# An unused table of 192 bytes ahead of the weight buffers: where the weights lie in SBUF

## The chip, the cores and the metric

The kernel runs on one core of a Trainium2 chip, in float32, one launch. The metric is the device time of the launch in microseconds (us). The numbers below come from the kernel's times and from one profiled execution of it.

## What is computed

Two transformer blocks over 256 tokens of width 1024. The first has chunked attention over 16 heads beside a gated linear recurrence, then a SwiGLU feed-forward; the second has four SwiGLU feed-forwards, a gated spatial mixing and a stick-breaking attention. Cut to its matrix products:

```python
u  = rmsnorm(x, g) @ w_in                       # 1024 x 7168
ya = chunked_band_attention(q, k, v) @ w_attn_out
yb = (rg_lru(conv(xr)) * gelu(gr)) @ w_rnn_out
h  = x + (g_a * ya + g_b * yb) @ w_o
gu = rmsnorm(h, g2) @ w_ffn_in                  # 1024 x 5632
h  = h + (silu(gu[:, :2816]) * gu[:, 2816:]) @ w_ffn_out
# second block: four more such feed-forwards, chunked_sgu (1024 x 4096, 2048 x 1024),
# k, v = rms_norm(x) @ w_kv, stick_breaking_attention(q, k, v) @ b_w_o, last rms_norm
```

## The kernel before

All weights pass through the core once. `PLAN` cuts them into 240 groups of 1 MB, each two chunks of 128 x 1024 floats. `load` (line 142) brings one group into one of three `raw` buffers by a DMA on SP's queue. `prep` (line 152) splits a chunk: ScalarE writes `h`, the rounded part (line 165), VectorE writes `l`, the rest (line 166), both as float32r. There are eight `h` and eight `l` buffers of 4096 bytes a partition; `prep` runs up to seven chunks ahead of the matmuls.

Activations are split the same way: into `xh` and `xl` (the normed input of a stage) and into the four `rr` tables (the input of an output projection). Each product of a chunk is three matmuls on line 213 (`mm3`, and the loops of `pe_nat` and `pe_rn`): h times h, h times l, l times h. They stand in two ways:

- `pe_k`, `pe_a` and `pe_r` **load the weights**, 128 x 128 of `h` or `l`, into the array and stream 256 columns of activations.
- `pe_nat` and `pe_rn` **stream the weights**, 512 columns of `h` or `l`, past 128 x 128 loaded activations. The feed-forwards' input projections (with the last one's output projection), the value projection and the spatial mixing's first half go this way. The stage of `kv_emit` loads weights in half of its matmuls and streams 256 columns of them in the other half.

The order is written by hand: each engine gets its instructions in the order of the code, and generators (`spawn`, `rounds`) put the work on finished stages between the chunks. TensorE reads a chunk once its `h` and `l` are ready, and ScalarE writes a buffer anew once the matmuls on its old content are done.

Every tile of the pool `const` gets its bytes of a partition in the order in which the code asks for it, rounded up to 32 bytes; the pools `raw` and `hl` follow behind it. So the sizes of the small tables ahead decide where the large buffers start. Before, these are the starting bytes in each partition, and what is left over a multiple of 512:

| tile | starts at | over a multiple of 512 |
|---|---|---|
| `x0` to `x3`, `xh`, `xl`, `rr0` to `rr3`, `sa` | 17408 to 74752 | 0 |
| `sb` to `sh`, `ident`, `ones` | 83072 to 132736 | 128 |
| `ntri`, `nones` (asked for after `setup`) | 136672, 137184 | 480 |
| three `raw` buffers of 8192 bytes | from 138816 | 64 |
| eight `h`, eight `l` buffers of 4096 bytes | from 163392, 196160 | 64 |

Every slice of these that a matmul reads starts a multiple of 512 bytes behind its tile's start.

Of the kernel before, what the change touches and what calls it, by code (L numbers as in the profile page):

```python
# [109 lines left out]
class Builder:  # L110
# [210 lines left out]
    def setup(self):  # L321
        nc, dram = self.nc, self.dram
        self.P = self.sb("par", [128, 224])[:, 0:NPAR]
        self.X = [self.sb(f"x{p}", [128, 2, 256]) for p in range(4)]
        self.XS = (self.sb("xh", [128, 8, 256], F32R), self.sb("xl", [128, 8, 256], F32R))
        self.RR = [self.sb(f"rr{i}", [128, 8, 256], F32R) for i in range(4)]
        self.SA = self.sb("sa", [128, 2080])[:, 0:8 * 259]
        self.SL = {c: self.sb("s" + c, [128, 2048]) for c in "bcdfgh"}
        self.ident = self.sb("ident", [128, 128])
        self.ones = self.sb("ones", [128, 128])  # L330
        self.mhalf = self.sb("mhalf", [128, 2])
        self.Rt = self.sb("rt", [128, 256])
        self.R1 = self.sb("r1t", [128, 256])
        self.Rkv = self.sb("rkv", [128, 256])
        self.rckv = self.sb("rckv", [128, 2])
        self.v2 = self.sb("v2", [128, 2])
        self.rc = self.sb("rc", [128, 2])
        self.tiny = self.sb("tiny", [128, 1])
        self.rc05 = self.sb("rc05", [128, 2])
        self.c8 = self.sb("c8", [128, 8])  # L340
        self.nc8 = self.sb("nc8", [128, 8])
        self.half = self.sb("half", [128, 24])
        self.sq = self.view("b", 4)
        nc.scalar.dma_start(self.P, dram["par"])
        x_load = lambda p: nc.sync.dma_start(self.X[p], dram["x"][:, 2 * p:2 * p + 2, :])
        for f in range(2):
            nc.sync.dma_start(self.X[0][:, f, :], dram["x"][:, f, :])
        self.warm_up()
        for g in range(2):
            t = self.rawp.tile([128, 2048], F32, tag="raw", name="raw")  # L350
            for c in range(2):
                if 2 * g + c:
                    x_load(2 * g + c)
                n = 512 if 2 * g + c == 0 else 1024
                for o in range(c * 1024, (c + 1) * 1024, n):
                    nc.sync.dma_start(t[:, o:o + n], dram["w"][g, :, o:o + n])
            self.raw[g] = t
        self.loads = 2
        self.load()
        self.gw = self.SL["h"].rearrange("p (a b) -> p a b", b=128)  # L360
        make_identity(nc, self.ident)
        nc.gpsimd.memset(self.ones, 1.0)
        nc.gpsimd.memset(self.mhalf, -0.5)
        nc.gpsimd.memset(self.tiny, 2.0 ** -115)
# [1041 lines left out]
```

## Time and profile before

| | us |
|---|---|
| median of 3 runs | 1444.81 |
| lowest, highest of the 3 | 1444.66, 1446.23 |
| the profiled execution | 1445.04 |
| its span, first to last instruction | 1443.3 |
| TensorE busy in the span | 1431.0 |

The mean granted clock of TensorE over the span was 0.998 of its 2.4 GHz. The page and the views name an operation as line, engine, operation, result <- inputs. For a matmul the streamed operand stands before the loaded one: `wk<-xh,h` streams `xh` past loaded `h`, `wk<-h,xh` streams `h` past loaded `xh`. The duration of one matmul is longer than the distance to the next start, since matmuls are pipelined; the pace is read from starts, or from a piece of the chain of work: its length over its count.

### The profile page before, as it was taken

Reading aid. Unit: us, or ns where it says so; the run is one execution under the profiler, and the core shown is the slowest. Engines: PE = TensorE matmul, PEld = TensorE weight load, DVE = VectorE, ACT = ScalarE, POOL = GpSimd, SP = SyncE. Lnnn points to the kernel's source line nnn. Section 1 sums busy time; section 2 is a strip of 40 time slices with the busy share of each in tenths; the row PEclk is TensorE's granted clock in tenths of the full one; section 3 lists DMA queues with packets and bytes.
Section 4 is the critical chain, followed back from the end, with each engine's and each line's share of the span. In section 5 each row is a group of like instructions: output and inputs, shape, how many; then the busy total and the mean of one; then the engine's idle time right before and its main releaser. Section 6 shows DMA issues by size and latency. Waiting matters only on the chain.

```text
span 1443.3 us, 21730 instructions
## 1 busy us (share of the span) xinstructions
PE 1431.0 (99%) x9112; PEld 1277.2 (88%) x9112; DVE 875.1 (61%) x1102; ACT 732.0 (51%) x985; POOL 21.4 (1%) x57
## 2 busy tenths in 40 slices
PE   8999999999999999999999999999999999999998
PEld 8998989888888888898999888898888898888886
DVE  6976688655547555566775554457555477644453
ACT  5777465544445544455444544446444467544442
POOL 0000000000000000000000000000000000000000
PEclk9999999999999999999999999999999999999999
DMA  7555545554553545546444555545554542445440
GB/s 296 197 193 200 186 160 195 188 201 175 184 195 147 204 176 180 209 151 224 171 168 155 222 185 180 191 154 204 186 193 176 183 168 88 161 176 193 186 175 30
DMA packets 37602, 259.98 MB, mean 180 GB/s; under 512 B 4224, under 2 KB 4608, under 8 KB 7040
## 3 DMA queue, kind: packets, MB, share of 16 engines
q1 hardware_dynamic: 36288, 253.77, 48.3%
q0 software_dynamic: 1072, 4.72, 1.0%
q8 instruction: 71, 1.16, 0.3%
q14 instruction: 27, 0.22, 0.0%
q10 hardware_dynamic: 144, 0.10, 0.0%
HBM read 257.53 MB, written 1.05 MB: 179 GB/s over the span
## 4 chain that ended last, share of the span: by engine, by line
PE 97%; DVE 1%; DMA 0%; ACT 0%; issue 0%; POOL 0%; SPq 0%; POOLq 0%; DVEq 0%; ACTq 0%
PE wk L213 60%; PE acc L213 35%; PE wk L755 2%; DMA raw<-w 0%; DVE l L166 0%; PE acc L525 0%; ACT h L165 0%; DVE sd L275 0%; DVE sb L275 0%; PE wk L525 0%; POOL r1c L283 0%; ACT sf L1020 0%; DVE sf L1011 0%; ACT sd L1010 0%; DVE sa L747 0%
## 5 line engine op out<-in xcount | busy, mean ns | idle before, releaser
L166 DVE TENSOR_TENSOR l<-raw,h 128x1024 fp32r<-128x1024 f32 (+1 forms) x479 | 572.7, 1220 | 317.2 <-ACT h L165 316.7
L165 ACT ACTIVATE h<-raw 128x1024 fp32r<-128x1024 f32 (+1 forms) x479 | 495.3, 1053 | 303.5 <-PE wk L213 192.7
L213 PE MATMUL wk<-h,xh 128*128 128x512 f32 x912 | 361.9, 397 | 0.0
L213 PE MATMUL wk<-h,xl 128*128 128x512 f32 x912 | 359.6, 394 | 0.0
L213 PE MATMUL wk<-l,xh 128*128 128x512 f32 x912 | 359.2, 394 | 0.0
L213 PE MATMUL acc<-rr,h 128*128 128x256 f32 x2016 | 358.5, 281 | 0.0
L213 PEld LDWEIGHTS acc<-rr,h 128*128 128x128 f32 x2016 | 307.9, 188 | 3.6 <-issue 1.9
L213 PE MATMUL acc<-rr,l 128*128 128x256 f32 x1008 | 281.2, 279 | 0.0
L213 PEld LDWEIGHTS wk<-h,xl 128*128 128x128 f32 x912 | 171.8, 188 | 39.4
L213 PEld LDWEIGHTS wk<-l,xh 128*128 128x128 f32 x912 | 171.9, 189 | 37.2
L213 PEld LDWEIGHTS wk<-h,xh 128*128 128x128 f32 x912 | 171.9, 188 | 36.8
L213 PEld LDWEIGHTS acc<-rr,l 128*128 128x128 f32 x1008 | 190.0, 189 | 0.0
L213 PE MATMUL wk<-xh,h 128*128 128x256 f32 x512 | 145.5, 284 | 2.0 <-ACT h L165 2.0
L213 PE MATMUL wk<-xh,l 128*128 128x256 f32 x512 | 143.2, 280 | 1.0 <-DVE l L166 1.0
L213 PE MATMUL wk<-xl,h 128*128 128x256 f32 x512 | 143.0, 279 | 0.0
L213 PEld LDWEIGHTS wk<-xh,h 128*128 128x128 f32 x512 | 96.1, 188 | 4.6 <-ACT h L165 2.4
L213 PEld LDWEIGHTS wk<-xh,l 128*128 128x128 f32 x512 | 97.2, 190 | 1.4 <-DVE l L166 1.4
L213 PEld LDWEIGHTS wk<-xl,h 128*128 128x128 f32 x512 | 96.5, 188 | 0.2
L312 ACT ACTIVATE rr<-wk 128x512 fp32r<-128x512 f32 (+1 forms) x63 | 35.9, 569 | 113.9 <-PE wk L755 109.2
L313 DVE TENSOR_TENSOR rr<-wk,rr 128x512 fp32r<-128x512 f32 (+1 forms) x63 | 41.4, 657 | 77.8 <-ACT rr L312 77.8
L743 ACT ACTIVATE sg<-wk,rc 128x512 f32<-128x512 f32 (+1 forms) x48 | 30.8, 652 | 75.6 <-PE wk L213 67.8
L747 DVE SCALAR_TENSOR_TENSOR sa<-wk,rc,sg 128x512 f32<-128x512 f32 (+1 forms) x48 | 32.3, 706 | 53.7 <-PE wk L213 50.0
(256 smaller groups left out, 1167.3 us busy)
## 6 DMA issues: line engine op xcount, KB each, us to landing
raw<-w SPq DMA_DIRECT2D x237, 1024.0 KB, 4.8
sd<-bias POOLq DMA_DIRECT2D x8, 384.0 KB, 3.3
raw<-w SPq DMA_DIRECT2D x3, 512.0 KB, 7.7
sh<-gates SPq DMA_DIRECT2D x1, 1024.0 KB, 9.0
out<-sf SPq DMA_DIRECT2D x4, 256.0 KB, 2.2
x<-x SPq DMA_DIRECT2D x3, 256.0 KB, 6.9
raw<-w SPq DMA_DIRECT2D x2, 256.0 KB, 4.3
sa<-ws POOLq DMA_DIRECT2D x1, 512.0 KB, 5.3
```

Of the source, the lines that this page charges most:

```text
L165: nc.scalar.activation(h[:, s], raw[:, s], AF.Copy)
L166: nc.vector.tensor_tensor(l[:, s], raw[:, s], h[:, s].bitcast(F32), op=ALU.subtract)
L213: self.nc.tensor.matmul(out, lhsT, rhs, start=start, stop=stop, skip_group_check=True)
L312: self.nc.scalar.activation(zh, src, AF.Copy)
L313: self.nc.vector.tensor_tensor(zl, src, zh.bitcast(F32), op=ALU.subtract)
L743: nc.scalar.activation(SG[i][t][:, 0:w], src, AF.Silu, scale=self.rcol[:, t:t + 1])
L747: nc.vector.scalar_tensor_tensor(Z[i][t][:, 0:w], src, s, SG[i][t][:, 0:w], op0=ALU.mult, op1=ALU.mult)
L755: nc.tensor.transpose(bank[:, f, t * 128:(t + 1) * 128], Z[i][t][:, o:o + 128], self.ident)
```

## The change

One line in `setup` asks the pool `const` for a table of 48 floats a partition that nothing writes or reads:

```diff
         self.nc8 = self.sb("nc8", [128, 8])
         self.half = self.sb("half", [128, 24])
+        self.sb("gap", [128, 48])
         self.sq = self.view("b", 4)
```

No instruction is added, removed or moved: the rows of all five engines stand as before but for line numbers behind 342 and the numbers in names. Every tile that is asked for behind the table starts 192 bytes later:

| tile | starts at | over a multiple of 512 |
|---|---|---|
| `x`, `xh`, `xl`, `rr`, `sa`, `sb` to `sh`, `ident`, `ones` | as before | as before |
| `ntri`, `nones` | 136864, 137376 | 160 |
| three `raw` buffers | from 139008 | 256 |
| eight `h`, eight `l` buffers | from 163584, 196352 | 256 |

`identb`, `maskb` and the small tables of statistics behind them move by the same 192 bytes.

## Rows read from the trace of the kernel before

**Rows 1.** The page: busy time; TensorE's granted clock in 40 slices; the chain by engine.
```profile
PE 1431.0 (99%) x9112; PEld 1277.2 (88%) x9112; DVE 875.1 (61%) x1102; ACT 732.0 (51%) x985; POOL 21.4 (1%) x57
...
PEclk9999999999999999999999999999999999999999
...
PE 97%; DVE 1%; DMA 0%; ACT 0%; issue 0%; POOL 0%; SPq 0%; POOLq 0%; DVEq 0%; ACTq 0%
```

**Rows 2.** Groups of matmuls by form: names, loaded and streamed shape, count | busy, mean.
```profile
L213 PE MATMUL wk<-h,xh 128*128 128x512 f32 x912 | 361.9, 397 | 0.0
...
L213 PE MATMUL acc<-rr,h 128*128 128x256 f32 x2016 | 358.5, 281 | 0.0
...
L213 PE MATMUL wk<-xh,h 128*128 128x256 f32 x512 | 145.5, 284 | 2.0 <-ACT h L165 2.0
...
L213 PE MATMUL acc<-h,rr 128*128 128x512 f32 x176 | 57.7, 397 | 0.0
...
L213 PE MATMUL wk<-rr,h 128*128 128x256 f32 x192 | 33.3, 278 | 0.0
...
L213 PE MATMUL acc<-h,xh 128*128 128x512 f32 x64 | 25.5, 398 | 0.0
...
L213 PE MATMUL acc<-xh,h 128*128 128x256 f32 x64 | 18.4, 288 | 0.0
...
L213 PE MATMUL acc<-sb,sh 128*128 128x256 f32 x32 | 7.6, 379 | 0.0
```

**Rows 3.** The chain of work in order of time: start us, length us, what, count.
```profile
239.94 16.09 PE wk L213 x142
...
334.84 22.40 PE wk L213 x96
...
754.98 25.09 PE acc L213 x213
...
1324.09 21.97 PE wk L213 x96
```

**Rows 4.** Timeline of TensorE's matmuls around 186 us: start us, length us, what.
```profile
183.75 0.28 PE L213 MATMUL wk<-xh,h 128*128 128x256 f32 x1
...
186.02 0.28 PE L213 MATMUL wk<-xh,l 128*128 128x256 f32 x1
...
187.03 0.28 PE L213 MATMUL wk<-xh,l 128*128 128x256 f32 x1
...
188.44 0.28 PE L213 MATMUL wk<-xh,l 128*128 128x256 f32 x1
```

**Rows 5.** Timeline of TensorE's matmuls in the stage of `kv_emit`.
```profile
1162.24 0.28 PE L213 MATMUL acc<-l,rr 128*128 128x256 f32 x1
...
1162.71 0.28 PE L213 MATMUL acc<-h,rr 128*128 128x256 f32 x1
...
1163.18 0.39 PE L213 MATMUL acc<-rr,h 128*128 128x256 f32 x2
...
1163.52 0.28 PE L213 MATMUL acc<-h,rr 128*128 128x256 f32 x1
...
1164.20 0.40 PE L213 MATMUL acc<-rr,h 128*128 128x256 f32 x2
```

**Rows 6.** Timeline of TensorE's matmuls of the recurrence's gates, plain float32, first six.
```profile
46.51 1.46 PE L213 MATMUL acc<-sb,sh 128*128 128x256 f32 x6
```

**Rows 7.** Groups by line: the splits; busy, mean ns | idle before, what ended it.
```profile
L166 DVE TENSOR_TENSOR l<-raw,h 128x1024 fp32r<-128x1024 f32 (+1 forms) x479 | 572.7, 1220 | 317.2 <-ACT h L165 316.7
L165 ACT ACTIVATE h<-raw 128x1024 fp32r<-128x1024 f32 (+1 forms) x479 | 495.3, 1053 | 303.5 <-PE wk L213 192.7 <-PE acc L213 99.6 <-DMA raw<-w 9.8
```

**Rows 8.** TensorE's waits: us in total, times, longest us.
```profile
PE wk L213 <- ACT h L165: 2.0, 2, 1.1
...
PE wk L213 <- DVE l L166: 1.0, 2, 0.8
```

**Rows 9.** Timeline of the first microseconds: the first split of weights and its wait.
```profile
5.93 1.27 ACT L165 ACTIVATE h<-raw 128x512 fp32r<-128x512 f32 x2 [1.22 <-DMA raw<-w]
```

**Rows 10.** Groups of matmuls by form: a moved constant table as loaded operand.
```profile
L213 PE MATMUL wk<-rr,nones 128*128 128x256 f32 x20 | 4.0, 280 | 0.0
```

## The prediction, made before the result was known

> **What bounds the kernel now.** I read the page first, then the groups by form, then the chain of work and the timeline. TensorE is busy 1431.0 us of a 1443.3 us span and is 97% of the chain that ended last, at full clock in every slice [rows 1]. So only what changes the distance between two matmuls, or stops TensorE, can change the time. Its stops on the splits are small: 2.0 us on `h` and 1.0 us on `l` in the whole run [rows 8].
>
> The groups by form say which matmuls fill those 1431 us [rows 2]. Of 512 columns of streamed weights there are three groups of 912 (one stands in the rows; the other two have the same count), 176 with 88 of its `l` partner, and three of 64: 2736 + 264 + 192 = 3192. Of 256 columns of activations past loaded weights there are 2016 + 1008, three of 512, 192 + 96, and three of 64: 3024 + 1536 + 288 + 192 = 5040. Together 8232 of 9112. Their durations are no price, since they overlap.
>
> The price is the pace, and the chain shows that each kind has **two paces** [rows 3]. 512 columns: 22.40 us over 96 is 233.3 ns, in another feed-forward 21.97 over 96 is 228.9 ns. 256 columns: 25.09 us over 213 is 117.8 ns, elsewhere 16.09 over 142 is 113.3 ns. Both pairs lie 4.4 ns apart. At the full clock of 2.4 GHz 512 columns at one a cycle would be 213.3 ns and 256 would be 106.7 ns, so 16 to 20 and 7 to 11 ns of each distance are something else, and an operand's place in SBUF could be it. That is all the change can act on.
>
> **The change part by part.** The table adds no instruction and no transfer; no order, queue or wait is changed by the code. Its own cost is nothing. It moves five things.
>
> *Loaded weights (5040 matmuls) and streamed weights (3192).* Before, the weights lie 64 bytes past a multiple of 512 and the activations at 0. Does this offset set the pace? Three readings say not.
>
> First, the same instructions at the same offset run at both paces. In one group of the query and key projection 20 starts from 183.75 to 186.02 us lie 113.5 ns apart; after a short stop for six transposes, 12 starts from 187.03 to 188.44 lie 117.5 ns apart [rows 4]. Same tiles, same slices modulo 512, other pace. What differs is how the stretch began.
>
> Second, the stage of `kv_emit` swaps the roles within a chunk, so that first the loaded operand lies at 64 and the streamed one at 0, then the reverse. Streamed weights: 6 distances from 1163.52 to 1164.20, 113.3 ns; 4 from 1162.24 to 1162.71, 117.5 ns. Loaded weights just before: 3 distances from 1163.18 to 1163.52, 113.3 ns [rows 5]. Offsets of +64 and -64 between streamed and loaded operand give the same two paces.
>
> Third, the paces hold through long stretches that walk over many buffers: 213 matmuls with nothing but 117.8, 142 with 113.3 [rows 3].
>
> So I take the price per matmul at +256 (which is -256 as well, modulo 512) as what it is at +64 and -64: nothing. What the trace can't show is an offset of 256 itself, so I bound it. From below: every matmul at the fast pace of its kind. From above: every one at the slow pace. Fast: 3192 x 228.9 = 730.6 and 5040 x 113.3 = 571.0, together 1301.7 us. Slow: 3192 x 233.3 = 744.7 and 5040 x 117.8 = 593.7, together 1338.4 us. Before lies between, in a mixture; I put it at the middle, 1320.0, since the chain shows long pieces of each. So the bounds are -18.3 and +18.3 us, and the value I take is 0, by [rows 5], the nearest.
>
> *The splits* read `raw` and write `h` and `l`, all moved alike, so their offset to each other stays 0. Were ScalarE's 1053 ns or VectorE's 1220 ns to change by some per cent, the cover is their idle time: 303.5 us before `h`, of which 292.3 us waited for TensorE to free a buffer, and 317.2 us before `l` [rows 7]. 479 splits can each grow by some 0.6 us before that is gone. I take 0; the bounds are the 3.0 us that TensorE now waits [rows 8], in either direction.
>
> *The loads of weights* write 8192 bytes a partition at another offset. ScalarE waited 9.8 us in all for them [rows 7], most of it at other times than TensorE stopped; only at the start, 1.22 us before the first split [rows 9], is the wait on the path. Bounds -0.5 to +0.5 us, value 0.
>
> *`ntri` and `nones`* go from 480 to 160 past a multiple of 512. They serve 64 matmuls in the stick-breaking stage (20 of one group stand in the rows [rows 10]). By one pace step, 64 x 4.4 ns = 0.3 us either way; 0.
>
> *The small statistics* are columns of one or two floats; 0.
>
> The sum: 0, so the profiled execution's own 1445.04 us, of which 1.7 us lie around the span, stays. It stands 0.2 us above the median of the runs; I predict 1445.0.
>
> **The rivals.**
>
> *The stretches are dealt anew* (both signs). The pace is fixed when a stretch begins [rows 4], after a stop whose end is set by ScalarE, VectorE or a transfer. If any of these ends some ns earlier or later, stretches can change pace. One of 96 x 512 columns is worth 96 x 4.4 = 0.42 us, so a net seven of them must go one way to make 2.9 us. The feed-forwards repeat the same pattern (most show 22.40 for 96, the last one 21.97 [rows 3]), so several can go together. Against a large net: some would flip each way. Typical -8 or +8 us, 1437 or 1453; bounds as above, 1426.7 and 1463.3.
>
> *The offset is what the extra ns are* (faster). If at 64 the two operands disturb each other and at 256 they don't, the paces fall to the floor. The trace has one: the recurrence's gates, in plain float32, with both operands 128 past a multiple of 512. Six of them take 1.46 us; less the last one's 379 ns that is 1.08 over 5, 216 ns [rows 2, 6], which is 2.7 ns over 512 cycles. Then 512 columns cost 216.0 and 256 cost 106.7 + 2.7 = 109.3 ns: 3192 x (231.1 - 216.0) + 5040 x (115.6 - 109.3) = 48 + 32 = 80 us, a time of 1365. For it: something takes 16 to 20 ns from each. Against: the gates pass a column only every second cycle, which is enough of a difference by itself, and +64 and -64 cost the same. The Trainium skill ("TensorE: Matmul & The Clock Gate", "Back-to-back issue gap") gives N / 2.4 + 2.5 ns as the gap of a lone stream, 215.8 and 109.2 ns here; the gates' row agrees, the rows of the split matmuls don't, and by the page's figures alone the sum would be the same 1365 as an estimate.
>
> *The operands fall in step* (slower). A loaded 128 x 128 block has 512 bytes a partition. With 64 between them the two reads begin at different places of such a span; 256 may be a multiple of whatever span the memory is divided by (64 is less likely to be), so that both reads meet at one place and one waits. Price: one more step of 4.4 ns, the only step that the trace shows, for each matmul: 3192 x 4.4 = 14 us if it hits only streamed weights, 5040 x 4.4 = 22 us if only loaded ones, 36.6 us for both: 1459 to 1482. It decides the sign from 2.9 us, 0.35 ns a matmul. For it: the paces do come in steps, so something periodic is there. Against: the role swap in `kv_emit` changes nothing.
>
> *The table gets no bytes* and nothing moves: the same 1445.0. It gets them: the starting bytes differ by 192.
>
> **How the numbers follow.** A difference of 0.2%, 2.9 us, is about what a measurement of this kernel can tell from no change. No effect, stretches dealt about as before: 0.42. Dealt anew by more than 2.9 us: 0.14 faster, 0.14 slower. The floor or a part of it: 0.15. In step: 0.15. So faster 0.29, same 0.42, slower 0.29. The range takes the bounds of the dealing, 1426 to 1464, which also holds about half of the in-step case (streamed weights alone) and small parts of the floor case; left out are some 0.2. The likeliest case by itself would be 1442 to 1448.
>
> **What would show it.** Right: the chain has pieces of 113.3 and 117.8, 228.9 and 233.3 ns and no other, the stage of `kv_emit` shows the same distances in both roles, the idle time before the splits stays near 300 us each. Dealt anew: the same four paces, but other pieces have them (the 22.40 us of 96 becomes 21.97, or the reverse). Floor: 96 in 20.7 us, 213 in 23.3 us. In step: a fifth pace, 237.8 or 122.2 ns, and most likely only in one of the two roles. Wrong altogether would be a change in TensorE's stops or clock, since nothing here reaches them.

## The result and the profile after

The changed kernel takes 1453.28 us (median of 4 runs, 1453.07 to 1453.39), the kernel before in the same measurement 1444.77. The ratio is 1.0056, with a 95% interval of 1.0039 to 1.0074: slower by 0.6%, 8.5 us. The forecast was 1445.0, no change. The profiled execution takes 1453.28 us, its span is 1451.6.

The page of the kernel after, three lines as in [rows 1]:

```profile
PE 1440.4 (99%) x9112; PEld 1296.2 (89%) x9112; DVE 876.1 (60%) x1102; ACT 731.7 (50%) x985; POOL 22.4 (2%) x57
...
PEclk9999999999999999999999999999999999999999
...
PE 97%; DVE 1%; DMA 0%; ACT 0%; issue 0%; POOL 0%; SPq 0%; POOLq 0%; DVEq 0%; ACTq 0%
```

TensorE is busy 9.4 us longer with the same 9112 matmuls at the same clock, and its share of the chain is the same 97%. VectorE and ScalarE, which have slack, are within a microsecond of before. So the time went into TensorE's matmuls themselves, and not into a wait. Two more views bear that out. The groups by line of the two splits, and TensorE's waits on them (engine and line, waited for, us in total, times, longest), against [rows 7, 8]:

```profile
L166 DVE TENSOR_TENSOR l<-raw,h 128x1024 fp32r<-128x1024 f32 (+1 forms) x479 | 573.2, 1221 | 313.1 <-ACT h L165 312.9
L165 ACT ACTIVATE h<-raw 128x1024 fp32r<-128x1024 f32 (+1 forms) x479 | 495.0, 1053 | 300.9 <-PE wk L213 182.2 <-PE acc L213 104.0 <-DMA raw<-w 8.0
```

```profile
PE wk L213 <- ACT h L165: 1.1, 1, 1.1
...
PE wk L213 <- DVE l L166: 0.5, 1, 0.5
```

A split takes 1053 and 1221 ns, as before to a nanosecond, and its idle time is still about 300 us. TensorE's own waits on the splits fell from 3.0 to 1.6 us. The loads of 128 x 128 blocks into the array (PEld on the page), which overlap the matmuls, are busy 19 us longer, 1296.2 in place of 1277.2; whether that is a cause or a consequence of the new paces is not shown.

The chain of work in order of time (start us, length us, what, count) has the cause. The pieces answer to those of [rows 3]:

```profile
341.10 21.79 PE wk L213 x96
...
754.98 25.08 PE acc L213 x209
...
1333.04 21.76 PE wk L213 x96
```

The 96 matmuls that stream 512 columns of weights took 22.40 us (in the last feed-forward 21.97). Now they take 21.79 and 21.76: 227.0 and 226.7 ns for each, **less** than either pace of before. The same 25.1 us from 754.98 held 213 matmuls past loaded weights and now hold 209: 120.0 ns for each, **more** than either pace of before. Over the whole run, from the starts of all matmuls without a stop between them:

| | before | after |
|---|---|---|
| 256 columns, long stretches | 113.3 or 117.8 ns | 120.0 ns |
| 256 columns, mean | 115.9 ns | 119.9 ns |
| 512 columns, long stretches | 228.9 or 233.3 ns | 226.7 to 227.5 ns |
| 512 columns, mean | 230.9 ns | 227.3 ns |

5040 x 4.0 = +20.2 us and 3192 x -3.6 = -11.5 us make +8.7 us. The two profiled executions differ by 8.24. To within half a microsecond that is the whole result, as the difference of two effects of opposite sign.

In the stage of `kv_emit`, where both roles stream 256 columns, the timeline (start us, length us, what) shows one distance in place of the two of [rows 5]:

```profile
1171.07 0.28 PE L213 MATMUL acc<-rr,l 128*128 128x256 f32 x1
1171.19 0.40 PE L213 MATMUL acc<-rr,h 128*128 128x256 f32 x2
1171.43 0.28 PE L213 MATMUL acc<-rr,l 128*128 128x256 f32 x1
1171.55 0.28 PE L213 MATMUL acc<-h,rr 128*128 128x256 f32 x1
1171.67 0.28 PE L213 MATMUL acc<-l,rr 128*128 128x256 f32 x1
1171.79 0.40 PE L213 MATMUL acc<-h,rr 128*128 128x256 f32 x2
1172.03 0.28 PE L213 MATMUL acc<-l,rr 128*128 128x256 f32 x1
```

Eight distances from 1171.07 to 1172.03, 120 ns each, with weights loaded (`rr,h`) and with weights streamed (`h,rr`). So, as far as this stage shows, the sign of the effect goes with 256 or 512 columns and not with the role.

### The profile page after: what moved, and what is told of

The parts are those of the page before. It is cut to its first block, busy times and chain, and to the rows that moved or that the text cites. A ratio compares the mean times of both kernels' runs of the same rounds, so it can differ in the third digit from the quotient of the medians.

```text
span 1451.6 us, 21730 instructions
## 1 busy us (share of the span) xinstructions
PE 1440.4 (99%) x9112; PEld 1296.2 (89%) x9112; DVE 876.1 (60%) x1102; ACT 731.7 (50%) x985; POOL 22.4 (2%) x57
## 4 chain that ended last, share of the span: by engine, by line
PE 97%; DVE 1%; DMA 0%; ACT 0%; issue 0%; POOL 0%; SPq 0%; POOLq 0%; DVEq 0%; ACTq 0%
PE wk L213 59%; PE acc L213 36%; PE wk L756 2%; DMA raw<-w 0%; DVE l L166 0%; PE acc L526 0%; ACT h L165 0%; DVE sd L275 0%; DVE sb L275 0%; PE wk L526 0%; POOL r1c L283 0%; ACT sf L1021 0%; DVE sf L1012 0%; ACT sd L1011 0%; DVE sa L748 0%
## 5 line engine op out<-in xcount | busy, mean ns | idle before, releaser
L166 DVE TENSOR_TENSOR l<-raw,h 128x1024 fp32r<-128x1024 f32 (+1 forms) x479 | 573.2, 1221 | 313.1 <-ACT h L165 312.9
L165 ACT ACTIVATE h<-raw 128x1024 fp32r<-128x1024 f32 (+1 forms) x479 | 495.0, 1053 | 300.9 <-PE wk L213 182.2
L213 PE MATMUL acc<-rr,h 128*128 128x256 f32 x2016 | 370.1, 285 | 0.0
L213 PE MATMUL wk<-h,xh 128*128 128x512 f32 x912 | 357.5, 392 | 0.0
L213 PE MATMUL wk<-l,xh 128*128 128x512 f32 x912 | 355.2, 389 | 0.0
L213 PE MATMUL wk<-h,xl 128*128 128x512 f32 x912 | 355.1, 389 | 0.0
L213 PEld LDWEIGHTS acc<-rr,h 128*128 128x128 f32 x2016 | 315.2, 192 | 3.5 <-issue 1.9
L213 PE MATMUL acc<-rr,l 128*128 128x256 f32 x1008 | 285.3, 283 | 0.0
L213 PEld LDWEIGHTS acc<-rr,l 128*128 128x128 f32 x1008 | 193.2, 192 | 0.0
L213 PE MATMUL acc<-h,rr 128*128 128x512 f32 (+1 forms) x208 | 64.5, 378 | 0.0
```

The lines of the kernel that those rows point to most:

```text
L165: nc.scalar.activation(h[:, s], raw[:, s], AF.Copy)
L166: nc.vector.tensor_tensor(l[:, s], raw[:, s], h[:, s].bitcast(F32), op=ALU.subtract)
L213: self.nc.tensor.matmul(out, lhsT, rhs, start=start, stop=stop, skip_group_check=True)
```

## The experiments

Each run is compared with the kernel before, timed beside it (its medians were 1444.5 to 1445.0). **Distance** below is the start of the loaded operand less the start of the streamed one, in bytes of a partition modulo 256. With the weights at 64, as before, it is 64 where weights are loaded and 192 where they are streamed. With the weights at 256 it is 0 for both.

### Moving the activations too

The table stands ahead of `x0`, so that activations and weights all move by 192 bytes. Weights end at 256 as in the changed kernel, with the old distances.

```diff
+        self.sb("gap", [128, 48])
         self.X = [self.sb(f"x{p}", [128, 2, 256]) for p in range(4)]
...
-        self.sb("gap", [128, 48])
         self.sq = self.view("b", 4)
```

> The same table of 192 bytes, but asked for ahead of `x`, so that activations and weights both start 192 bytes later: activations at 192, weights at 256 past a multiple of 512, their distance 64 as before. Distance theory (the pace follows from the distance between the streamed and the loaded operand): the four paces of before, 113.3 and 117.8, 228.9 and 233.3 ns, and about 1445 us, at most 3 us off since stretches can be dealt anew. Place theory (it follows from where the weights themselves start): one pace each as with the change, 120.0 and 226.7 ns, and about 1453 us.

Measured: 1444.72 us, ratio 1.0001 (0.9991 to 1.0010). The chain has the old pieces:

```profile
334.38 22.40 PE wk L213 x96
...
754.97 25.09 PE acc L213 x213
```

So this place of the weights is nothing by itself. What counts is where they lie relative to the activations.

### Moving only the split weights

The table becomes a pool of its own between `raw` and the `h` and `l` buffers. `raw`, `ntri`, `nones` and the statistics stay where they were.

```diff
-        self.sb("gap", [128, 48])
...
+            tc.tile_pool(name="gap", bufs=1) as gapp, \
             tc.tile_pool(name="hl", bufs=NB) as hlp, \
...
+        gapp.tile([128, 48], F32, tag="gap", name="gap")
```

> The unused table lies between the buffers of raw and of split weights: `h` and `l` at 256, `raw` and all small tables where they were before. Distance theory and place theory: 120.0 and 226.7 ns, about 1453 us, since TensorE reads `h` and `l` alone. Theory of the splits (the moved `raw`, or the distance between `raw` and `h`, changes the splits or the loads, and by that when TensorE starts): the paces of before and 1445 us, or a third time with splits that differ from 1053 and 1221 ns.

Measured: 1453.28 us, ratio 1.0057 (1.0043 to 1.0072), the whole effect:

```profile
341.56 21.79 PE wk L213 x96
...
754.96 25.08 PE acc L213 x209
```

The loads of weights, the splits' reads and the constant tables have no part in it.

### The `rr` tables at the old distance, the normed input at the new one

The table stands behind `xl` and no longer in its old place: `rr`, `sa` and the weights move, `xh` and `xl` don't.

```diff
         self.XS = (self.sb("xh", [128, 8, 256], F32R), self.sb("xl", [128, 8, 256], F32R))
+        self.sb("gap", [128, 48])
```

> The table lies between `xl` and `rr0`: `xh` and `xl` stay at 0, the `rr` tables go to 192, weights to 256. So matmuls of weights with `xh` and `xl` have a distance of 256, those with `rr` one of 64. Distance theory: 120.0 and 226.7 ns with `xh` and `xl`; the output projections with `rr` go back to 113.3 or 117.8 ns, the last projection's streamed weights to 229 to 233 ns. 3312 x (120.0 - 115.6) = 14.7 us less than with the change, 264 x 4.4 = 1.2 us more: about 1440 us, faster than both kernels. Place theory: 1453 us.

Measured: 1442.62 us, ratio 0.9986 (0.9976 to 0.9995), faster than before, but by less than expected.

```profile
338.73 21.77 PE wk L213 x96
...
754.99 25.09 PE acc L213 x213
```

Each product has the pace of its own distance, as expected: `xh` and `xl` at 0 stream at 226.7 ns, and the `rr` products at 64 are back at 113.3 and 117.8. What fell short is the mixture of these two. In before 1597 of 3140 such matmuls in stretches of at least 20 ran at 117.8, here 2434. These 837 x 4.4 ns = 3.7 us are most of what the profiled execution lacks: it took 1444.40 us, 4.4 more than expected. Why the median of its runs lies 1.8 us below that is not shown. The last two experiments come back to the mixture.

### Five other distances

Only the size of the table in the changed kernel is another. It puts the weights 128, 320, 192 and 448 bytes past a multiple of 512; for 0 the table goes, and three small tables become parts of one, which saves 64 bytes.

```diff
-        self.sb("gap", [128, 48])
+        self.sb("gap", [128, 16])
```

> A table of 64 bytes in place of 192: weights at 128, activations at 0. It maps the distance. If two reads that begin in step are what makes 120.0 ns, 128 keeps them apart: paces like those of 64, about 1445 us. If the paces go with the distance by steps of 64 bytes, 128 lies between: some pace from 117.8 to 120.0 ns for 256 columns and from 226.7 to 228.9 ns for 512, about 1449 us.

```diff
-        self.sb("gap", [128, 48])
+        self.sb("gap", [128, 64])
```

> A table of 256 bytes: weights at 320, 256 more than before. If the distance counts modulo 256, this is the kernel before: paces 113.3 and 117.8, 228.9 and 233.3 ns, 1445 us. If it counts modulo 512 (the size of a loaded block), the paces may be others, and the time differs from 1445 by more than 3 us.

```diff
-        self.mhalf = self.sb("mhalf", [128, 2])
+        small = self.sb("small", [128, 5])
+        self.mhalf = small[:, 0:2]
...
-        self.rckv = self.sb("rckv", [128, 2])
+        self.rckv = small[:, 2:4]
...
-        self.tiny = self.sb("tiny", [128, 1])
+        self.tiny = small[:, 4:5]
...
-        self.sb("gap", [128, 48])
```

> Three small tables (`mhalf`, `rckv`, `tiny`) are columns of one, which saves 64 bytes: weights at 0, all operands at multiples of 512, distance 0. Modulo 256: as with the change, 120.0 and 226.7 ns, 1453 us. Modulo 512: another pace; if reads that begin in step are what costs, then more than 120.0 ns and over 1460 us.

```diff
-        self.sb("gap", [128, 48])
+        self.sb("gap", [128, 32])
```

> A table of 128 bytes: weights at 192. If the distance counts modulo 256 and its sign doesn't matter, 192 is -64 and gives the paces of before and 1445 us (the role swap in the stage of the key and value projection, where both signs showed 113 and 118 ns, speaks for it). If the sign matters, a time that can lie anywhere from 1440 to 1470 us.

```diff
-        self.sb("gap", [128, 48])
+        self.sb("gap", [128, 96])
```

> A table of 384 bytes: weights at 448, the distance -64 modulo 512. Modulo 256 it is the same as 192 and gives that run's paces and time to within 3 us. Modulo 512 with the sign of no weight it is the kernel before: 1445 us, whatever 192 gives.

Measured, with the two kernels for comparison:

| weights past a multiple of 512 | us | ratio to before |
|---|---|---|
| 64 (before) | 1444.8 | 1 |
| 320 | 1444.63 | 0.9998 (0.9989 to 1.0007) |
| 0 | 1453.75 | 1.0059 (1.0044 to 1.0074) |
| 256 (the change) | 1453.28 | 1.0056 (1.0039 to 1.0074) |
| 192 | 1461.11 | 1.0112 (1.0095 to 1.0128) |
| 448 | 1460.67 | 1.0108 (1.0093 to 1.0123) |
| 128 | 1465.63 | 1.0143 (1.0128 to 1.0158) |

The rows come in pairs 256 bytes apart. The distance counts **modulo 256**, as expected for 320, 0 and 448, and the kernel before stood at the best of these four places. For 128 neither of the two expectations held: 1445 and 1449 us were expected. The chain bears the pairs out. Its pieces of 256 columns behind 755 us, first of the weights at 320, then at 0, then at 448, are 117.8, 120.0 and 117.8 ns a matmul:

```profile
754.89 25.20 PE acc L213 x214
...
754.89 25.20 PE acc L213 x210
...
754.99 25.09 PE acc L213 x213
```

The pieces of both kinds, first of the weights at 128, then at 192:

```profile
341.08 22.32 PE wk L213 x96
...
758.83 21.24 PE acc L213 x177
```

```profile
339.51 22.40 PE wk L213 x96
...
755.53 24.50 PE acc L213 x208
```

At 128: 232.5 and 120.0 ns. At 192: 233.3 and 117.8 ns, with few stretches at 113.3 and none at 228.9. So +64 and -64 are not the same in time: with weights at 64 both roles have a fast and a slow pace, with weights at 192 (each distance with its sign turned) 512 columns show only the slow one and 256 columns nearly so (253 of 4721 matmuls in long stretches are fast). For 256 columns both signs show the same two paces; whether the sign itself or the way stretches begin makes the fast one rare at 192 is not shown. The sum holds here too. At 192 the mean is 117.5 ns over 256 columns and 233.3 over 512: 5040 x 1.6 + 3192 x 2.4 = 15.7 us, measured 16.1.

### A distance of its own for each role

If each product's pace goes by its own distance, the feed-forwards' input projections should stand at 0 and the products past loaded weights at 64. `xh` and `xl` get two places 64 bytes apart in a larger tile. A stage that is a feed-forward writes and reads the second place (`XM`), every other stage the first. Weights are at 320, `rr` at 256 past a multiple of 512.

```diff
-        self.XS = (self.sb("xh", [128, 8, 256], F32R), self.sb("xl", [128, 8, 256], F32R))
+        th, tl = self.sb("xh", [128, 2064], F32R), self.sb("xl", [128, 2096], F32R)
+        at = lambda t, o: t[:, o:o + 2048].rearrange("p (a b) -> p a b", b=256)
+        self.XS = (at(th, 0), at(tl, 48))
+        self.XM = (at(th, 16), at(tl, 0))
...
-                    self.group(kk, lambda c, h, l, s: self.pe_nat(h, l, s[2], self.XS, banks), mid=mid, end=end)
+                    self.group(kk, lambda c, h, l, s: self.pe_nat(h, l, s[2], self.XM, banks), mid=mid, end=end)
```

> The distance is chosen for each role: the normed input of a stage has two places, 64 bytes apart. For the five feed-forwards' input projections (2640 matmuls that stream 512 columns of weights) the distance between loaded and streamed operand is 0 modulo 256, for all matmuls that load weights it stays 64 as before. Theory (the distance modulo 256 sets the pace of each matmul by itself): 2640 matmuls go from a mean of 230.9 to 227.3 ns, -9.5 us, the rest stays: 1435, every long stretch of the feed-forwards' input projections at 226.7 ns, those past loaded weights at 113.3 and 117.8. Rival (what counts is the sum over the run or another tile, and faster stretches here are paid by slower ones elsewhere, as the one that left the rr tables at 64 but showed more of 117.8): 814 matmuls more at 117.8, +3.6 us: 1439. If the place in SBUF and not the distance counts, 1445.

Measured: 1440.08 us, ratio 0.9967 (0.9955 to 0.9979). It beats both kernels. First two pieces of before, then the same two here:

```profile
334.84 22.40 PE wk L213 x96
357.24 5.47 PE acc L213 x48
```

```profile
335.57 21.77 PE wk L213 x96
357.35 5.65 PE acc L213 x48
```

The streamed weights gave what was expected: their mean fell from 231.2 to 227.0 ns, 2640 x 4.2 = 11 us. But the 48 matmuls behind them, whose operands lie as before, went from 5.47 to 5.65 us, 117.8 ns in place of 114. The `rr` products lost 1.5 ns in the mean, 3312 x 1.5 = 5 us. Together that is 6 us less, and the two profiled executions differ by 5.6. The rival of this run was right: stretches are dealt anew.

The next two kernels are the same with 96 and with 32 bytes in place of 64 for the loaded weights (two places 96 or 32 bytes apart, and the tables behind shifted to fit, which the cuts leave out).

```diff
...
-        self.XS = (at(th, 0), at(tl, 48))
-        self.XM = (at(th, 16), at(tl, 0))
+        self.XS = (at(th, 0), at(tl, 40))
+        self.XM = (at(th, 24), at(tl, 0))
...
```

> As the one with two places, but 96 bytes in place of 64 for all matmuls that load weights; the feed-forwards' input projections at distance 0. Theory A (the pace changes smoothly with the distance, so 96 lies between 64, mean 115.9 ns, and 128, mean 118.6 ns): 117.2 ns, 5040 x 1.3 = +6.6 us against the one with 64: 1442. Theory B (each distance picks its pace from a grid, and 96 can pick the 113.3 ns alone): 5040 x -2.6 = -13 us: 1422. A new pace, neither 113.3, 117.8 nor 120.0, would speak for A.

```diff
...
-        self.XS = (at(th, 0), at(tl, 48))
-        self.XM = (at(th, 16), at(tl, 0))
+        self.XS = (at(th, 0), at(tl, 56))
+        self.XM = (at(th, 8), at(tl, 0))
...
```

> As the one with two places, but 32 bytes in place of 64 for all matmuls that load weights; the feed-forwards' input projections at distance 0. Theory A (smooth): 32 lies between 0, 120.0 ns, and 64, mean 115.9 ns: 118.0 ns, 5040 x 2.1 = +10.6 us against the one with 64: 1446. Theory B (a grid of paces, one or two of them for each distance): 113.3 alone would give 1422, 117.8 alone 5040 x 1.9 = +9.6 us, 1445, and the stretches would show no pace between.

Measured: 1448.42 us, ratio 1.0028 (1.0016 to 1.0039), with 96, and 1447.85, ratio 1.0021 (1.0011 to 1.0030), with 32. The piece of 48 matmuls, first with 96, then with 32:

```profile
359.84 5.70 PE acc L213 x48
```

```profile
360.68 5.68 PE acc L213 x48
```

Neither theory of these two runs holds. 32 bytes give 118.3 ns, about what a smooth change between 0 (120.0) and 64 (115.9 in the mean) would. 96 bytes give 118.7 and in about a third of the matmuls some 117.4, in the mean 118.2, where a smooth change to 128 asked for 117.2. There are paces between those of the other distances, so it is no short list of paces either. What is shown is that 64 lies in a dip: the means at 32 and 96 are 118.3 and 118.2 ns, at 64 they are 115.9 in before and 116.9 in the kernel with two places. Outside the feed-forwards these two kernels also stream 512 columns, at the distances 160 (the one with 96) and 224 (the one with 32). What the runs say of each distance, in ns of long stretches (a dash: no long stretch):

| distance | 256 columns, weights loaded | 512 columns, weights streamed |
|---|---|---|
| 0 | 120.0 | 226.7 to 227.5 |
| 32 | 118.3 | - |
| 64 | 113.3 or 117.8 | 233.3 |
| 96 | 118.7, a third 117.3 to 117.6 | - |
| 128 | 118.7 or 120.0 | 232.4, some 233.3 |
| 160 | - | 233.3 to 233.5 |
| 192 | 117.8, few 113.3 | 228.9 or 233.3 |
| 224 | - | 233.2 to 233.4 |

### What picks one of the two paces

With two paces at one distance, what picks? I went through the stretches past loaded weights that follow a stretch of streamed weights, each of at least 12 matmuls. In before, 12 of 12 behind one at 233.3 ns run at the fast pace, and of 10 behind one at 228.9 ns seven do. In the two kernels that stream at 0 and load at 64, 41 of 41 behind a stretch at 226.7 to 227.5 ns run at the slow pace. Yet the pace of the stretch ahead is not the rule: with the weights at 192, 22 of 22 behind one at 233.3 ns are slow. What does go with the pace is the first step out of the streamed stretch. In all six kernels here that load at 64 (the last run below among them), the distance from the last streamed matmul to the first one past loaded weights is 226 or 227 ns ahead of each of the 60 slow stretches, and 230 to 236 ns ahead of each of the 59 fast ones. So the choice stands with the first matmul of a stretch; what makes it is not shown by that. The last run tries to change this without touching a distance. In three feed-forwards one matmul at the start of each group of the output projection is cut in two; the fourth feed-forward is left as it was.

```diff
+            if cut and o == 0 and not first:
+                out = accs[0][:, 0, :]
+                self.mm(out, h[:, s], zh, False, False)
+                self.mm(out[:, 0:cut], h[:, s], zl[:, 0:cut], False, False)
+                self.mm(out[:, cut:256], h[:, s], zl[:, cut:256], False, False)
+                self.mm(out, l[:, s], zh, False, last)
+                continue
...
+                cut = {"f0": 128, "f1": 120, "f2": 124}.get(n, 0)
```

> The kernel with two places for the normed input (1440.1), and in three feed-forwards one of the 256-column matmuls at the start of each group of the output projection (the second of its first chunk, 9 groups of 48 matmuls each) is cut in two: 128 + 128 columns in the first feed-forward, 120 + 136 in the second, 124 + 132 in the third; the fourth is left whole. Question: what sets which of the two paces of distance 64 a stretch takes. In the kernel before, every long stretch past loaded weights that followed a stretch at 233.3 ns ran at 113 to 114 ns, and with two places every one that followed a stretch at 226.7 ns ran at 117.8. Theory A (the moment within a short cycle at which a stretch begins decides, and it is kept): an odd piece shifts that moment, and in at least one of the three the stretches of 48 go from 5.65 to 5.47 us behind the cut, while the fourth feed-forward stays at 5.65; if in all three, 3 x 432 x 4 ns = -5 us, less 27 more matmuls at some 60 ns, +1.6 us: 1436.5. Theory B (the pace belongs to the distances of the two roles together, not to how a stretch begins): 5.65 in all four and 1440.1 + 1.6 = 1441.7.

Measured: 1438.30 us, ratio 0.9957 (0.9942 to 0.9972), the lowest median of all kernels here. Pieces of the chain of the first, the third and the fourth feed-forward (49 and 25 where one matmul was cut):

```profile
370.23 21.77 PE wk L213 x96
392.00 5.58 PE acc L213 x49
...
877.73 5.58 PE acc L213 x49
...
883.75 2.93 PE acc L213 x25
...
1065.23 5.66 PE acc L213 x48
```

With a cut, 49 matmuls take less time than 48 without (5.58 against 5.66 us). In the first two feed-forwards all groups go to about 114 ns behind the cut. With 124 + 132 columns six of the nine groups do: 5.58 for the first group of a pair, but in three of the four pairs the second stays slow, 2.93 for 25, 117 ns. The fourth, uncut, stays at 117.9. So how a stretch begins decides its pace, and the stretch keeps it, as in the first theory of this run; that a moment within a short cycle is what counts, as that theory has it, is not shown. The gain over the kernel without cuts is 1.8 us by the medians, where 3.4 were expected for all three: 24 of 27 groups turn fast, 24 x 48 x 4 ns = 4.6 us, and a cut costs some 0.11 us (5.58 against the 5.47 us of a fast group of 48 in before), not 0.06, 3.0 us in all. That gain in time is not clear of noise: the interval of the kernel without cuts, 0.9955 to 0.9979, overlaps this one, and the two profiled executions differ by 0.7 us. It is the pieces of the chain that show the effect.

## Where the prediction was right and where wrong, point by point

The time lies inside the range, above the forecast by 8.3 us, but by luck: the reason given for the forecast was wrong.

- **What bounds the kernel**: right. TensorE's busy time grew by 9.4 us and the run by 8.5. Only the distance between matmuls changed, not a stop.
- **The splits, the loads, `ntri`, the statistics at nothing**: right. Moving `h` and `l` alone gives the whole 8.5 us, and the idle time before the splits stayed at 313 and 301 us.
- **"So I take the price per matmul at +256 as what it is at +64 and -64: nothing"**: this is the step that failed. It took an offset that the trace didn't hold to be worth what two others were. The price measured is +4.0 ns for each of 5040 matmuls and -3.6 ns for each of 3192.
- **The second reading, the role swap in `kv_emit`**, carried that step, and it does not carry it. It showed that 64 and 192 (which is -64) can both give 113.3 and 117.8 ns in a dozen matmuls, each role with the sign it had, and all of them matmuls of 256 columns. The kernel with the weights at 192 turns both signs: it runs nearly always at the slow paces and takes 1461.11 us. Two places on a curve say nothing of a third, and these two weren't equal in time either.
- **The first and the third reading**, that one distance has two paces, that the start of a stretch picks one and the stretch keeps it, are right; the cut matmuls show it. What did not follow from them is that the distance has no say: it sets which paces there are, and the start picks among them.
- **The bounds of -18.3 and +18.3 us** were made of paces that belong to the distances of before, 64 and 192. The result lies inside them for another reason: the new paces lie outside both pairs (120.0 above 117.8, 226.7 below 228.9), and two terms of +20.2 and -11.5 us happen to cancel in part. With the weights at 128, where both are slow, the time is 1465.63, 21 us up and past the upper bound.
- **The rival "The operands fall in step"** had the right quantity: the distance, with 256 a multiple of a span. That one of two reads waits, as it has it, no run shows. The weights at 0 and 256 agree, and so do 64 with 320 and 192 with 448. Its price was off. It took one more step of 4.4 ns up, 122.2 and 237.8 ns; the 256 columns went up to 120.0 and the 512 columns went down. That falling in step could be the *fastest* place for 512 columns was in none of my cases. Its ground against, that the role swap changes nothing, was the same mistake again.
- **The floor**: wrong. At no distance tried do the paces come near 216.0 and 109.3 ns. The Trainium skill ("TensorE: Matmul & The Clock Gate", "Back-to-back issue gap") has N / 2.4 + 2.5 ns for an isolated matmul, 215.8 and 109.2 ns here; the lowest paces that any long stretch here shows for the split matmuls are 226.7 and 113.3.
- **The stretches dealt anew**: not what the change did, since its pieces have other paces than the four of before. But the mechanism is there: it took some 5 us from the kernel with two places.

## What to carry to other kernels

Where TensorE is the bound, the place of its two operands in SBUF relative to each other, modulo 256 bytes, is a setting to be tried. In this kernel it is worth 1.4% between the worst and the best of one offset for all weights, and 1.9% with an offset for each role and the starts steered (1465.6 against 1438.3). A table put in or taken out ahead of large buffers moves it unseen, so that an unrelated edit can look like a gain or a loss of half a per cent; compare starting bytes before explaining such a difference. And when a forecast rests on "no effect", ask whether the trace holds two values of the thing that changes: if not, the bounds have to come from somewhere else than the rows at the one value.

## What the runs showed of the hardware

- The pace of matmuls in float32r with a new loaded block each depends on the distance between loaded and streamed operand modulo 256 bytes, between 113.3 and 120.0 ns for 256 columns, 226.7 and 233.5 for 512. The best distance for 512 columns, 0, is the worst for 256. Of the six distances tried or met with 512 columns, 0 alone gives 227 ns and 192 alone has a second pace below 232. Why the sign turns between 256 and 512 columns was not settled, nor what is read at which moment.
- The Trainium skill ("TensorE: Matmul & The Clock Gate", "Step-by-step: what each phase is for") says that loading the next block of weights takes no read bandwidth from the running matmul. The trace shows that the two are not independent: the same instructions with one operand 192 bytes further take 120.0 in place of 113.3 to 117.8 ns. Whether it is read bandwidth that they share, the runs don't show.
- One distance can have two paces, and one cut matmul at the start of a stretch moves some 48 matmuls behind it from 117.8 to 114 ns. Behind streamed weights at 227 ns an uncut stretch with loaded weights at 64 is slow, 41 times of 41 in two kernels; the step of 226 or 227 ns between the two stretches, in place of 230 to 236, tells it in advance.
